# Gate/up projection: the even blocks 2 to 8 take three of their eight k-pairs by seven products

## The chip, the cores and the metric

The kernel runs on one core of a Trainium2 chip. The metric is the device time of one execution in microseconds (us); of several runs the median is given. TensorE (PE in the profile) multiplies, VectorE (DVE), ScalarE (ACT) and GpSimd (POOL) do the element-wise work, and SyncE (SP) issues most of the transfers from memory.

## The reference

One decoder layer on 256 tokens of width 2048, all in float32. Only the two feed-forward parts are touched by the change; each has gate and up projections of 2048 x 5632 and a down projection of 5632 x 2048.

```
def swiglu(x, w_gate, w_up, w_down):
    return (jax.nn.silu(x @ w_gate) * (x @ w_up)) @ w_down

def reference(x, ...):
    x = x + 0.5 * swiglu(rms_norm(x, ffn1_norm), ffn1_w_gate, ffn1_w_up, ffn1_w_down)
    ...   # projection w_in, gated linear attention, dilated attention, projection w_out
    x = x + 0.5 * swiglu(rms_norm(x, ffn2_norm), ffn2_w_gate, ffn2_w_up, ffn2_w_down)
    return x
```

## The kernel before

**Numbers.** Each float32 operand is split into a high and a low part (`wh`, `wl` for weights, `hh`, `hl` for activations), and a product is the sum of high x high, high x low and low x high: three matmuls. `split` is one ScalarE copy (L115, writes the high part) followed by one VectorE subtraction (L116, writes the low part), so every weight passes through both engines before TensorE can use it.

**Tiling of gate and up.** The 5632 columns are 11 blocks of 512 columns of gate and 512 of up (`b` = 0 to 10). The 2048 rows are 16 tiles of 128, taken two at a time: 8 k-pairs to a block, here called pairs 0 to 7. One transfer of 1 MB (L221, on SP's queue) brings one pair's weights into a buffer `raw`; there are three such buffers, so the transfer for a pair is issued when VectorE and ScalarE are done with the pair three before it. Weight tiles `wh`, `wl` have `WBUF` = 4 buffers each.

**A plain pair** is two weight tiles, so two L115 and two L116 of 128x1024, and 24 matmuls of 512 columns: two row tiles, two token halves, gate and up, three matmuls each.

**A pair by seven products** treats two row tiles by two token halves times two row tiles by gate and up as a 2 x 2 product of blocks and takes 7 instead of 8 block products: 21 matmuls. For it `seven` prepares four weight tiles in the steps "plain" (the sum L242, two additions L245 into `room["more"]`, and the split of the middle two), "last" (a split of 128x512 into the single pair of tiles `swh`, `swl`), "sums" (the split of what L242 wrote), and "more" (the split of what both L245 wrote, by one ScalarE copy). All of them are VectorE and ScalarE work. Seven sums of products end in banks `ms`, which `fold` adds up after the block's last such pair (L490 on ScalarE, L491, L492, L493 on VectorE), and `evac` takes the block's result out (L456, L458, L459 on VectorE, L457 on ScalarE, then the 32x32 transposes L130, small transfers L137 on GpSimd's queue, and the split into `uh`, `ul`).

**Which pairs.** A text per block says it, `s` for a plain pair and `g` for one by seven products; `_order` numbers the `g` ones first:

```
FF_SEVEN = range(1, 11)
FF_THREE = range(1, 10, 2)
FF_ORDERS = [_order("ssgsggss" if b in FF_THREE else "ssgssgss" if b in FF_SEVEN else "ssssssss") for b in range(FF // 512)]
```

So block 0 is plain, the odd blocks 1 to 9 have three pairs by seven products (pairs 2, 4 and 5), and the even blocks 2 to 10 two (pairs 2 and 5). The accumulator banks change sides from block to block.

**What sets the order.** `weights()` keeps two to three weight tiles prepared ahead of their use; `later` holds pieces of other work that are handed out step by step. The program's builder then orders the instructions of each engine by a planned time line of its own. In the trace VectorE's instructions start in exactly the order of its list, so one that waits holds up all behind it.

Of the kernel before, what the change touches and what calls it, by code (L numbers as in the profile page):

```python
# [28 lines left out]
EPS = 1e-6  # L29
WBUF = 4  # L30
FF_SEVEN = range(1, 11)
FF_THREE = range(1, 10, 2)
TAIL = 4
WARM = 10
GH, GDK, GDV, RANK = 4, 128, 256, 16
# [4 lines left out]
def _order(text):  # L40

    seven, plain = iter(range(text.count("g"))), iter(range(text.count("g"), len(text)))
    return [(next(seven), True) if c == "g" else (next(plain), False) for c in text]


FF_ORDERS = [_order("ssgsggss" if b in FF_THREE else "ssgssgss" if b in FF_SEVEN else "ssssssss") for b in range(FF // 512)]
DOWN_ORDERS = [_order("ssssssgssgssgsgsgsgsss"), _order("sgsssgssgssgssgsgsssss")]
# [947 lines left out]
```

## Time and profile before

| | |
|---|---|
| median of 3 runs (lowest to highest) | 1713.23 us (1711.72 to 1714.13) |
| the profiled execution: its time, its span | 1712.98 us, 1711.2 us |
| granted TensorE clock | 0.999 |
| TensorE busy | 1701.1 us, 99%, 7944 records |
| VectorE busy | 1451.1 us, 85%, 1775 instructions |
| ScalarE busy | 964.8 us, 56% |
| GpSimd busy | 506.4 us, 30% |
| gate/up blocks 1 to 9, first feed-forward part | about 52 to 411 us of the span |
| gate/up blocks 1 to 9, second feed-forward part | about 1088 to 1446 us of the span |

A busy time is the time in which at least one instruction of the engine was in execution; matmuls overlap, so TensorE's busy time says little, and the spacing of their starts says more. Times in the rows below count from the start of the span. A row of the time line has the start, the duration, the engine, the line of the kernel, the operation, what it writes and reads, the shapes, a count, and in brackets the idle time of its engine before it and what ended that. `PE`, `DVE`, `ACT`, `POOL` and `SPq` are TensorE, VectorE, ScalarE, GpSimd and SyncE's queue.

### The profile page before, as it was taken

How to read it: one execution, taken by the hardware profiler on the slowest of the kernel's cores; microseconds unless marked ns; L12 is line 12 of the kernel's file. 1: busy time of each engine (PE TensorE's matmuls, PEld its weight loads, DVE VectorE, ACT ScalarE, POOL GpSimd, SP SyncE). 2: the span in 40 equal slices, each digit the busy share in tenths (PEclk: the TensorE clock that was granted, in tenths of full speed). 3: DMA queues.
4: the chain of work that ended last, by engine and by line, in shares of the span. 5: the costliest groups of instructions: out<-in, count | busy, mean ns of one | idle time of the engine just before them, and what ended most of it. 6: DMA issues, size and time to landing. Idle time of an engine off the chain costs nothing.

```text
span 1711.2 us, 22342 instructions
## 1 busy us (share of the span) xinstructions
PE 1701.1 (99%) x7944; PEld 1480.4 (87%) x7944; DVE 1451.1 (85%) x1775; ACT 964.8 (56%) x1195; POOL 506.4 (30%) x1002
## 2 busy tenths in 40 slices
PE   9999999999999999999999999999999999999999
PEld 7888888888888888888888888888888888888887
DVE  6989999999899788577865788899998999898876
ACT  7656565565555555564654555556555655555453
POOL 0333334343500511064250033343333333420000
PEclk9999999999999999999999999999999999999999
DMA  8566656566665656567564457666666666665654
GB/s 342 213 227 225 224 209 235 209 238 213 237 247 222 216 203 243 195 230 242 191 208 170 152 193 261 227 224 222 231 224 228 227 213 220 223 250 225 242 203 148
DMA packets 85809, 378.63 MB, mean 221 GB/s; under 512 B 21393, under 2 KB 38801, under 8 KB 42689
## 3 DMA queue, kind: packets, MB, share of 16 engines
q1 hardware_dynamic: 50864, 350.25, 57.2%
q0 software_dynamic: 34112, 25.88, 5.4%
q8 instruction: 62, 1.02, 0.2%
q10 hardware_dynamic: 720, 1.07, 0.2%
q14 instruction: 51, 0.41, 0.1%
HBM read 354.57 MB, written 4.19 MB: 210 GB/s over the span
## 4 chain that ended last, share of the span: by engine, by line
PE 92%; DMA 3%; DVE 3%; POOL 2%; issue 1%; ACT 0%; SPq 0%; DVEq 0%; ACTq 0%; POOLq 0%
PE acc L284 20%; PE acc L286 20%; PE acc L282 20%; PE acc L308 5%; PE acc L309 5%; PE acc L307 5%; PE tp L286 4%; PE tp L284 4%; PE tp L282 4%; DVE wl L116 1%; PE tp L309 1%; PE tp L308 1%; PE tp L307 1%; DMA hh<-us 1%; POOL hh L137 1%
## 5 line engine op out<-in xcount | busy, mean ns | idle before, releaser
L115 ACT ACTIVATE wh<-raw 128x1024 fp32r<-128x1024 f32 (+2 forms) x610 | 631.1, 1048 | 443.5 <-PE acc L286 194.2
L116 DVE TENSOR_TENSOR wl<-raw,wh 128x1024 fp32r<-128x1024 f32 (+1 forms) x608 | 732.2, 1218 | 147.9 <-ACT wh L115 145.3
L137 POOL DMA_DIRECT2D xs<-us x704 | 344.5, 497 | 545.9 <-DVE us L130 289.9
L286 PE MATMUL acc<-wh,hl 128*128 128x512 f32 x1192 | 359.8, 381 | 0.0
L284 PE MATMUL acc<-wl,hh 128*128 128x512 f32 x1192 | 358.9, 381 | 0.1
L282 PE MATMUL acc<-wh,hh 128*128 128x512 f32 x1192 | 349.0, 381 | 2.2 <-ACT wh L115 1.9
L282 PEld LDWEIGHTS acc<-wh,hh 128*128 128x128 f32 x1192 | 225.0, 189 | 36.4 <-ACT wh L115 3.0
L284 PEld LDWEIGHTS acc<-wl,hh 128*128 128x128 f32 x1192 | 225.3, 189 | 33.0 <-issue 0.7
L286 PEld LDWEIGHTS acc<-wh,hl 128*128 128x128 f32 x1192 | 225.6, 190 | 32.1 <-DVE hl L551 0.2
L115 ACT ACTIVATE wh<-xs 128x1024 fp32r<-128x1024 f32 x100 | 105.6, 1056 | 104.1 <-DVE xs L245 33.1
L116 DVE TENSOR_TENSOR wl<-xs,wh 128x1024 fp32r<-128x1024 f32 x100 | 120.8, 1218 | 2.4 <-ACT wh L115 2.4
L284 PE MATMUL acc<-wl,uh 128*128 128x512 f32 x384 | 117.4, 380 | 0.4 <-DVE wl L116 0.4
L286 PE MATMUL acc<-wh,ul 128*128 128x512 f32 x384 | 117.0, 379 | 0.0
L282 PE MATMUL acc<-wh,uh 128*128 128x512 f32 x384 | 112.2, 380 | 0.7 <-ACT wh L115 0.7
L137 POOL DMA_DIRECT2D hh<-us x128 | 62.2, 505 | 128.5 <-DVE us L130 68.2
L242 DVE TENSOR_TENSOR xs<-raw 128x1024 f32<-128x1024 f32 x50 | 61.3, 1225 | 29.7 <-DMA raw<-in_w_ff_dram 29.7
L282 PEld LDWEIGHTS acc<-wh,uh 128*128 128x128 f32 x384 | 72.3, 189 | 12.4 <-ACT wh L115 2.3
L284 PEld LDWEIGHTS acc<-wl,uh 128*128 128x128 f32 x384 | 72.3, 189 | 11.8 <-DVE wl L116 1.8
L286 PEld LDWEIGHTS acc<-wh,ul 128*128 128x128 f32 x384 | 72.6, 189 | 10.3
L245 DVE TENSOR_TENSOR xs<-xs,raw 128x512 f32<-128x512 f32 x100 | 68.7, 687 | 0.4
L282 PE MATMUL tp<-wh,hh 128*128 128x512 f32 x200 | 61.6, 379 | 0.0
L286 PE MATMUL tp<-wh,hl 128*128 128x512 f32 x200 | 59.5, 379 | 0.0
(325 smaller groups left out, 2474.7 us busy)
## 6 DMA issues: line engine op xcount, KB each, us to landing
raw<-in_w_ff_dram SPq DMA_DIRECT2D x175, 1024.0 KB, 5.1
raw<-in_w_dn_dram SPq DMA_DIRECT2D x88, 1024.0 KB, 4.9
raw<-in_w_mix_dram SPq DMA_DIRECT2D x48, 1024.0 KB, 4.9
raw<-in_w_out_dram SPq DMA_DIRECT2D x16, 1024.0 KB, 4.9
xs<-us POOLq DMA_DIRECT2D x704, 16.0 KB, 4.0
xs<-in_x_dram SPq DMA_DIRECT2D x2, 1024.0 KB, 9.3
xs<-in_x_dram POOLq DMA_DIRECT2D x2, 1024.0 KB, 5.5
hh<-us POOLq DMA_DIRECT2D x128, 16.0 KB, 3.8
```

Of the source, the lines that this page charges most:

```text
L115: nc.scalar.activation(dst_h, src, AF.Copy)
L116: nc.vector.tensor_sub(dst_l, src, dst_h.bitcast(F32))
L137: nc.gpsimd.dma_start(dst[32 * q:32 * q + 32, ..., r * n:(r + 1) * n], src[32 * r:32 * r + 32, ..., q * n:(q + 1) * n])
L242: nc.vector.tensor_add(room["sum"], b1, mid)
L245: nc.vector.tensor_add(room["more"][:, j, :], b, raw[:, 1, j, :])
L282: nc.tensor.matmul(ps[j], lhsT=sh, rhs=alt(wh[:, j, :]), start=first and i == 0, stop=False)
L284: nc.tensor.matmul(ps[j], lhsT=sh, rhs=alt(wl[:, j, :]), start=False, stop=False)
L286: nc.tensor.matmul(ps[j], lhsT=sl, rhs=alt(wh[:, j, :]), start=False, stop=last and i == len(ws) - 1)
L307: nc.tensor.matmul(bank, lhsT=a[0], rhs=alt(ws[0][:, j, :]), start=start, stop=False)
L308: nc.tensor.matmul(bank, lhsT=a[0], rhs=alt(ws[1][:, j, :]), start=False, stop=False)
L309: nc.tensor.matmul(bank, lhsT=a[1], rhs=alt(ws[0][:, j, :]), start=False, stop=stop)
```

## The change

The set of blocks with three such pairs becomes 1 to 9, so blocks 2, 4, 6 and 8 also take pair 4 by seven products. That is four pairs in each of the two feed-forward parts, eight in all.

```
-FF_THREE = range(1, 10, 2)
+FF_THREE = range(1, 10)
```

In the built program TensorE has 24 matmuls fewer, VectorE 40 instructions more and ScalarE 16 more; the transfers of SP and GpSimd are the same in number. The builder also orders VectorE's list anew, in the blocks that had three before as well. Two places of it follow, both in block 5 of the first feed-forward part (an odd block, three such pairs before and after). The numbers behind the names count buffers.

The first place is VectorE's work for pair 5, the last of the three, from its sum L242 to its last split ("more", the second `wl<-xs_78` after the two L245). Before:

```order
L242 TENSOR_TENSOR xs_78<-raw_2110 128x1024
L245 TENSOR_TENSOR xs_78<-xs_78,raw_2110 128x512
L116 TENSOR_TENSOR wl_2116<-raw_2110,wh_2115 128x1024
L245 TENSOR_TENSOR xs_78<-xs_78,raw_2110 128x512
L116 TENSOR_TENSOR swl_511<-raw_2110,swh_510 128x512
L116 TENSOR_TENSOR wl_2134<-xs_78,wh_2133 128x1024
L116 TENSOR_TENSOR ul_126<-xs_78,uh_125 128x4x128
L116 TENSOR_TENSOR wl_2144<-xs_78,wh_2143 128x1024
```

The same place after:

```order
L242 TENSOR_TENSOR xs_78<-raw_2122 128x1024
L116 TENSOR_TENSOR wl_2116<-xs_78,wh_2115 128x1024
L116 TENSOR_TENSOR wl_2128<-raw_2122,wh_2127 128x1024
L245 TENSOR_TENSOR xs_78<-xs_78,raw_2122 128x512
L116 TENSOR_TENSOR swl_511<-raw_2122,swh_510 128x512
L116 TENSOR_TENSOR wl_2146<-xs_78,wh_2145 128x1024
L245 TENSOR_TENSOR xs_78<-xs_78,raw_2122 128x512
L116 TENSOR_TENSOR ul_126<-xs_78,uh_125 128x4x128
L116 TENSOR_TENSOR wl_2156<-xs_78,wh_2155 128x1024
```

The second L245 moved back behind the split of the sums: one instruction (`ul`) stands between it and the split that needs its result, where three stood before. (`wl_2116<-xs_78` in the second row is pair 4's "more", which comes after pair 5's L242 now.)

The second place is VectorE's work at the end of the block, from pair 7's splits to L242 of the next block's pair 2. The buffer that this L242 reads (`raw_2334` before, `raw_2346` after) is the one that pair 7 held, three pairs earlier. Before:

```order
L116 TENSOR_TENSOR wl_2163<-raw_2150,wh_2162 128x1024
L491 TENSOR_TENSOR xs_78<-xs_78,acc_2017 128x512
L116 TENSOR_TENSOR wl_2175<-raw_2172,wh_2174 128x1024
L492 TENSOR_TENSOR xs_78<-xs_78,acc_2018 128x512
L116 TENSOR_TENSOR wl_2195<-raw_2172,wh_2194 128x1024
L493 TENSOR_TENSOR xs_78<-xs_78,acc_2016 128x2x512
L116 TENSOR_TENSOR wl_2215<-raw_2212,wh_2214 128x1024
L116 TENSOR_TENSOR wl_2231<-raw_2212,wh_2230 128x1024
L242 TENSOR_TENSOR xs_78<-raw_2334 128x1024
```

After:

```order
L116 TENSOR_TENSOR wl_2175<-raw_2162,wh_2174 128x1024
L116 TENSOR_TENSOR wl_2187<-raw_2184,wh_2186 128x1024
L491 TENSOR_TENSOR xs_78<-xs_78,acc_2029 128x512
L116 TENSOR_TENSOR wl_2207<-raw_2184,wh_2206 128x1024
L492 TENSOR_TENSOR xs_78<-xs_78,acc_2030 128x512
L116 TENSOR_TENSOR wl_2227<-raw_2224,wh_2226 128x1024
L493 TENSOR_TENSOR xs_78<-xs_78,acc_2028 128x2x512
L116 TENSOR_TENSOR wl_2243<-raw_2224,wh_2242 128x1024
L242 TENSOR_TENSOR xs_78<-raw_2346 128x1024
```

L491 and L492 moved one place back, so that L492 now stands between pair 7's last split, which frees the buffer, and the L242 that waits for it to be filled again. In blocks 3 to 9 of the first part and 4 to 9 of the second, pair 5's "more" follows its second L245 with `ul` alone between, and at the ends of the same blocks L492 stands behind pair 7's last split. At the ends of blocks 1 and 2 (1 to 3 in the second part) the order is still that from before.

## Prediction

> **What bounds the kernel now.** I read the page's busy shares first, then the windows of single blocks, then VectorE's time line at a block's end. The first fence has lines of the page (groups end with: busy us, mean ns of one | idle time before them). It shows a TensorE that is hardly ever idle and a VectorE at 85%; that is an average over stages, so the gate/up blocks have to be looked at alone.
>
> ```profile
> PE 1701.1 (99%) x7944; PEld 1480.4 (87%) x7944; DVE 1451.1 (85%) x1775; ACT 964.8 (56%) x1195; POOL 506.4 (30%) x1002
> L115 ACT ACTIVATE wh<-xs 128x1024 fp32r<-128x1024 f32 x100 | 105.6, 1056 | 104.1 <-DVE xs L245 33.1
> L242 DVE TENSOR_TENSOR xs<-raw 128x1024 f32<-128x1024 f32 x50 | 61.3, 1225 | 29.7 <-DMA raw<-in_w_ff_dram 29.7
> L245 DVE TENSOR_TENSOR xs<-xs,raw 128x512 f32<-128x512 f32 x100 | 68.7, 687 | 0.4
> ```
>
> The next fence has four windows. The first two run from TensorE's first low-part matmul of block 5 to that of block 6, and on to block 7's. The last two run from VectorE's L242 of pair 2 in block 5 to that of block 6, and on to block 7's.
>
> ```profile
> core 0: us, PE busy (x) PEld busy (x) DVE busy (x) ACT busy (x) POOL busy (x), PEclk, DMA share, GB/s
> 211.81:251.31 39.50, 39.50 (x185) 34.59 (x183) 37.48 (x42) 24.79 (x28) 15.63 (x32) 1.00 0.64 226
> 251.31:291.45 40.14, 40.14 (x187) 35.15 (x186) 36.66 (x43) 21.90 (x25) 15.66 (x32) 1.00 0.64 224
> ...
> 209.19:250.22 41.03, 41.03 (x191) 35.91 (x191) 39.01 (x45) 25.43 (x29) 15.63 (x32) 1.00 0.64 222
> 250.22:289.00 38.78, 38.78 (x181) 33.97 (x180) 35.31 (x39) 21.41 (x24) 15.66 (x32) 1.00 0.64 227
> ```
>
> TensorE needs 39.50 us for an odd block (183 matmuls) and 40.14 for an even one (186): 0.216 us each, without a stop. VectorE needs 41.03 us for an odd block, longer than TensorE, and 38.78 for an even one. So VectorE falls behind by 41.03 - 39.50 = 1.53 us in each odd block and makes up for it in the even one. TensorE leads the kernel only because every second block lets VectorE recover.
>
> The reason for the 41.03 is in VectorE's time line at the end of block 5 (start, duration, instruction, idle time before it).
>
> ```profile
> 237.27 0.69 DVE L116 TENSOR_TENSOR ul<-xs,uh 128x512 fp32r<-128x512 f32 x1
> 237.88 1.22 DVE L116 TENSOR_TENSOR wl<-xs,wh 128x1024 fp32r<-128x1024 f32 x1
> 239.01 2.35 DVE L116 TENSOR_TENSOR wl<-raw,wh 128x1024 fp32r<-128x1024 f32 x2
> 241.28 0.68 DVE L491 TENSOR_TENSOR xs<-xs,acc 128x512 f32<-128x512 f32 x1
> 241.88 1.22 DVE L116 TENSOR_TENSOR wl<-raw,wh 128x1024 fp32r<-128x1024 f32 x1
> 243.01 0.69 DVE L492 TENSOR_TENSOR xs<-xs,acc 128x512 f32<-128x512 f32 x1
> 243.61 1.22 DVE L116 TENSOR_TENSOR wl<-raw,wh 128x1024 fp32r<-128x1024 f32 x1
> 244.74 1.22 DVE L493 TENSOR_TENSOR xs<-xs,acc 128x1024 f32<-128x1024 f32 x1
> 245.88 2.36 DVE L116 TENSOR_TENSOR wl<-raw,wh 128x1024 fp32r<-128x1024 f32 x2
> 250.22 1.23 DVE L242 TENSOR_TENSOR xs<-raw 128x1024 f32<-128x1024 f32 x1 [1.98 <-DMA raw<-in_w_ff_dram]
> ```
>
> The 1.98 us are the only wait in that stretch; the work is 41.03 - 1.98 = 39.05 us, 0.45 less than TensorE's 39.50. The wait is a loop of VectorE's own: the split at 243.61 frees pair 7's buffer at 244.83, the next transfer into it lands 5.4 us later, and in between VectorE has 3.4 us of work. A later VectorE frees the buffer later, so the wait doesn't shrink when VectorE is behind. In a row, instructions start 1.14 us (128x1024) and 0.60 us (128x512) apart.
>
> The Trainium skill (VectorE: DVE Perf Modes, the section on the TRN2 errata) gives an fp32 add of N columns (N + 151)/0.96 ns, 691 and 1224 ns. The rows' single durations agree (687, 1225), but in a row the starts are closer; by the page an odd block's 44 instructions would take about 42.8 us (an estimate) instead of the 39.05 seen, and the loss below would be some 50 us. The trace decides, and the sum goes by 39.05.
>
> **How much room there is.** I call "lead" the time from L242 of a block's pair 2 on VectorE to TensorE's first low-part matmul (L284) of that block. The next rows give it for block 5 of the first part and block 2 of each part, and the first use of pair 6's low part.
>
> ```profile
> 209.19 1.23 DVE L242 TENSOR_TENSOR xs<-raw 128x1024 f32<-128x1024 f32 x1 [0.47 <-DMA raw<-in_w_ff_dram]
> 211.81 0.38 PE L284 MATMUL acc<-wl,hh 128*128 128x512 f32 x1
> 241.38 0.38 PE L284 MATMUL acc<-wl,hh 128*128 128x512 f32 x1
> ...
> 90.23 1.23 DVE L242 TENSOR_TENSOR xs<-raw 128x1024 f32<-128x1024 f32 x1 [1.31 <-DMA raw<-in_w_ff_dram]
> 92.02 0.38 PE L284 MATMUL acc<-wl,hh 128*128 128x512 f32 x1
> ...
> 1126.07 1.23 DVE L242 TENSOR_TENSOR xs<-raw 128x1024 f32<-128x1024 f32 x1 [1.36 <-DMA raw<-in_w_ff_dram]
> 1127.58 0.38 PE L284 MATMUL acc<-wl,hh 128*128 128x512 f32 x1
> ```
>
> Block 5 has a lead of 2.62 us. Pair 6's first low part is ready at 239.01 + 1.22 = 240.23 and used at 241.38, 1.15 us later. A block with three such pairs therefore needs a lead of 2.62 - 1.15 = 1.47 us, or TensorE waits. Block 2, the first that changes, has 1.79 in the first part and 1.51 in the second: just enough.
>
> **The change part by part.**
>
> TensorE: 24 matmuls fewer; per block 40.14 - 39.50 = 0.64 us, eight blocks, 5.1 us less.
>
> VectorE: 40 instructions more, five for each new pair, which turn an even block's work into an odd one's, 39.05 us. Every block from 2 to 9 then has 39.50 us of TensorE against 39.05 us of VectorE and its waits. More than 0.45 us of waits per block is lost, with no lighter block behind it to win it back.
>
> First wait, L242 at the block's end. In the eight odd blocks 3 to 9 of both parts it was (the row of 250.22 above is the eighth):
>
> ```profile
> 170.42 1.23 DVE L242 TENSOR_TENSOR xs<-raw 128x1024 f32<-128x1024 f32 x1 [1.70 <-DMA raw<-in_w_ff_dram]
> 330.68 1.23 DVE L242 TENSOR_TENSOR xs<-raw 128x1024 f32<-128x1024 f32 x1 [2.63 <-DMA raw<-in_w_ff_dram]
> 409.29 1.22 DVE L242 TENSOR_TENSOR xs<-raw 128x1024 f32<-128x1024 f32 x1 [1.41 <-DMA raw<-in_w_ff_dram]
> 1206.18 1.22 DVE L242 TENSOR_TENSOR xs<-raw 128x1024 f32<-128x1024 f32 x1 [1.51 <-DMA raw<-in_w_ff_dram]
> 1285.23 1.22 DVE L242 TENSOR_TENSOR xs<-raw 128x1024 f32<-128x1024 f32 x1 [1.31 <-DMA raw<-in_w_ff_dram]
> 1365.02 1.22 DVE L242 TENSOR_TENSOR xs<-raw 128x1024 f32<-128x1024 f32 x1 [1.47 <-DMA raw<-in_w_ff_dram]
> 1444.89 1.23 DVE L242 TENSOR_TENSOR xs<-raw 128x1024 f32<-128x1024 f32 x1 [1.70 <-DMA raw<-in_w_ff_dram]
> ```
>
> The mean is 13.71 / 8 = 1.71 us. It stays where the end of the block keeps its order. Where L492 now stands inside the loop, 0.60 us more work covers it: 1.11. But with L492 gone from before the split, pair 6's buffer and pair 7's are freed 1.14 + 0.60 + 1.14 = 2.88 us apart instead of 3.47 (244.83 less the end of the two splits from 239.01), and transfers close behind each other land late:
>
> ```profile
> L221 SPq DMA_DIRECT2D raw<-in_w_ff_dram x74: 327/328/328, 66.8 to 430.9; - x74
> 66.78 2.67 SPq L221 DMA_DIRECT2D raw<-in_w_ff_dram  x2
> raw<-in_w_ff_dram SPq DMA_DIRECT2D x1, 1024.0 KB, 5.7
> ...
> raw<-in_w_ff_dram SPq DMA_DIRECT2D x16, 1024.0 KB, 5.0
> ```
>
> The first row says that an issue takes 0.33 us; the second is two issues, so 2.67 - 0.33 = 2.34 us apart; the third is what the later of them took until it landed, the fourth the median of 16 transfers in blocks 5 and 6. So the wait lies between 1.11 and 1.71, and 1.30 is taken, nearer the lower end, as 2.88 lies between a spacing that cost 0.7 us and one that cost next to nothing.
>
> Second wait, ScalarE in the middle of pair 5. "More" needs the second L245 (0.69 us), then ScalarE's copy (1.06), then VectorE. That is 1.75 us and two hand-overs. One shows where VectorE waits for a copy at the end of block 4 (the copy ends at 206.40 + 1.06 = 207.46, the split starts at 207.49):
>
> ```profile
> 206.40 1.06 ACT L115 ACTIVATE wh<-raw 128x1024 fp32r<-128x1024 f32 x1 [1.53 <-PE acc L286]
> 207.49 1.23 DVE L116 TENSOR_TENSOR wl<-raw,wh 128x1024 fp32r<-128x1024 f32 x1 [0.76 <-ACT wh L115]
> ```
>
> With 0.03 for each it is 1.81 us, and with one `ul` between (0.60 + 0.60) VectorE has only 1.20 us to fill it and waits 0.61. At pair 4's "more" an L242 lies between (1.74), another 0.07: 0.68 in all, in blocks 3 to 9 (4 to 9 in the second part); 0.07 alone in the block before these. Its ends are nothing, if the copy starts sooner than I think, and 1.06, the whole copy. As it lies ahead of pair 6, the needed lead becomes 1.47 + 0.68 = 2.15.
>
> SP's and GpSimd's transfers are the same, and PSUM's fold and evacuation keep their distance, as VectorE is later and TensorE not; I cost them at nothing. If `ul` had to wait for GpSimd's transfers, the price would go to the second wait.
>
> The sum: block 2 loses 39.05 + 1.71 + 0.07 - 39.50 = 1.33 us of lead in the first part and 1.26 in the second, whose block 3 loses 1.33. Each later block loses 39.05 + 0.68 + 1.30 - 39.50 = 1.53. First part: 1.79 - 1.33 - 6 x 1.53 = -8.72 at block 9, where 2.15 are needed: TensorE waits 10.87. Second: 1.51 - 1.26 - 1.33 - 5 x 1.53 = -8.73: it waits 10.88. Block 10 keeps its two such pairs and VectorE recovers there. Together 21.75 of waits against 5.1 saved: +16.6 us. The profiled execution took 1712.98 us (span 1711.2), 0.25 below the median of 1713.23; with the median the forecast is 1729.8.
>
> **The rivals.**
>
> TensorE stays the bound (0.07). The saving is kept whole if a block's waits come to less than 0.45 us, for example if L242's wait only looks long because VectorE, four weight tiles ahead, had to wait there anyway. 1713.2 - 5.1 = 1708.1, faster. For it: at the end of block 5 VectorE is at its furthest ahead. Against it: block 6 started with 1.53 us less lead, and all eight waits are over 1.3. The Trainium skill (DMA: Bandwidth & Descriptors, "Rules for kernel authors") speaks for this rival: a transfer that is issued early, with work between it and its wait, overlaps its fixed cost. The trace agrees in part only: 3.4 us of work lie over a 5.4 us round trip, and 1.98 us stay bare.
>
> Break-even (0.10). The shortest wait, 1.31, shortened by the whole 0.60, and no ScalarE wait: 0.26 lost per block, 4 to 6 us of stalls in all against 5.1 saved, 1713.
>
> VectorE leads, but without the ScalarE wait (0.15): each block loses 0.85 and the lead needed is 1.47. First part -0.32 + 1.26 + 6 x 0.85 = 6.0, second -0.04 + 2.52 + 4.25 = 6.7, less 5.1: 1720.9.
>
> It gets worse (0.10). With the longest L242 wait (2.63 - 0.60 = 2.03) in each of the eleven later blocks the loss is 2.26 instead of 1.53 each, 8.0 us on top: 1737.8.
>
> **How the numbers follow.** The forecast's case, VectorE the bound with both waits, has 0.58: 1729.8, from 1723 to 1737. What a measurement of this kernel can tell from no change is about 0.2%, 3.4 us. Faster by more: the first rival, 0.07. Same: the break-even case, 0.10. Slower: 0.58 + 0.15 + 0.10 = 0.83. The range reaches from 1717, below the case without the ScalarE wait, to 1739, above the case of the longest L242 waits; 0.17 lies below it.
>
> **What would show it.** In the profile after: blocks 4 to 9 take about 41.0 us each on both engines; TensorE waits some 1.5 us per block, ended by VectorE's or ScalarE's splits at pairs 4 to 6; L242 of pair 2 still waits 1.1 to 1.7 us; "more" of pair 5 waits 0.6 us for ScalarE. Blocks of 39.5 us and no waits on TensorE would prove the forecast wrong; blocks near 40.3 would say that the ScalarE wait isn't there.

## The result and the profile after

The changed kernel took 1726.66 us (median of 6 runs, 1723.98 to 1728.39) and the kernel before, on the same chip, 1712.79 us (6 runs, 1711.68 to 1714.13): a ratio of 1.0082, with a 95% interval of 1.0072 to 1.0093, so 13.9 us slower. The prediction was 1729.8 us, slower. The profiled execution took 1728.39 us, with a span of 1726.6 us; before it was 1712.98 and 1711.2. The medians and ratios of this document are over executions at full speed: of the seven of the kernel e1 below, two are left out (2226.09 us at a granted clock of 0.752, and 7877.36 us), and one of eighteen of the kernel before beside it (3362.31 us).

The page's lines that answer to the first fence of the prediction:

```profile
PE 1704.2 (99%) x7920; PEld 1471.8 (85%) x7920; DVE 1481.9 (86%) x1815; ACT 970.1 (56%) x1211; POOL 506.4 (29%) x1002
L115 ACT ACTIVATE wh<-xs 128x1024 fp32r<-128x1024 f32 x116 | 122.5, 1056 | 165.2 <-DVE xs L245 119.7
L242 DVE TENSOR_TENSOR xs<-raw 128x1024 f32<-128x1024 f32 x58 | 70.8, 1220 | 25.5 <-DMA raw<-in_w_ff_dram 25.4
L245 DVE TENSOR_TENSOR xs<-xs,raw 128x512 f32<-128x512 f32 x116 | 79.2, 683 | 0.2
```

TensorE is still "99% busy", because the ends of its matmuls are modelled; that number hides the whole loss. What moved is ScalarE's idle time before the copies that wait for an L245: 119.7 us, where it was 33.1; that idle time costs nothing by itself, but VectorE's split behind such a copy comes later by it. L242's wait for raw transfers fell in total (25.4 after 29.7), though there are more of them.

The same four windows as before: two from TensorE's first low-part matmul of block 5 to that of blocks 6 and 7, two from VectorE's L242 of pair 2 to the next.

```profile
core 0: us, PE busy (x) PEld busy (x) DVE busy (x) ACT busy (x) POOL busy (x), PEclk, DMA share, GB/s
212.49:253.35 40.86, 40.24 (x185) 34.61 (x184) 37.93 (x44) 23.08 (x27) 15.65 (x32) 1.00 0.65 221
253.35:295.18 41.83, 40.36 (x184) 34.03 (x183) 39.94 (x45) 24.00 (x29) 15.66 (x32) 1.00 0.62 212
211.22:253.25 42.03, 41.41 (x191) 35.64 (x190) 39.10 (x44) 23.63 (x27) 15.65 (x32) 1.00 0.65 220
253.25:294.25 41.00, 39.53 (x180) 33.31 (x179) 39.11 (x45) 23.45 (x28) 15.66 (x32) 1.00 0.62 213
```

TensorE's blocks are now as long as VectorE's (40.86 and 41.83 against 42.03 and 41.00), and no longer 39.50. VectorE works 39.1 us in each and waits for the rest. Its time line shows both waits, at pair 5's "more" and at the next L242:

```profile
238.74 0.69 DVE L245 TENSOR_TENSOR xs<-xs,raw 128x512 f32<-128x512 f32 x1
239.34 0.69 DVE L116 TENSOR_TENSOR ul<-xs,uh 128x512 fp32r<-128x512 f32 x1
240.63 1.22 DVE L116 TENSOR_TENSOR wl<-xs,wh 128x1024 fp32r<-128x1024 f32 x1 [0.60 <-ACT wh L115]
...
249.78 1.22 DVE L116 TENSOR_TENSOR wl<-raw,wh 128x1024 fp32r<-128x1024 f32 x1
253.25 1.23 DVE L242 TENSOR_TENSOR xs<-raw 128x1024 f32<-128x1024 f32 x1 [2.26 <-DMA raw<-in_w_ff_dram]
```

And TensorE's time line shows where it stops in that block, at pair 5's last products and the first of pair 6:

```profile
240.65 0.48 PE L307 MATMUL acc<-wh,uh 128*128 128x512 f32 x1 [0.37 <-ACT wh L115]
241.59 0.70 PE L282 MATMUL acc<-wh,hh 128*128 128x512 f32 x2 [0.24 <-ACT wh L115]
```

The idle times in these two rows are too small, again because ends are modelled. Counted from the starts instead (what exceeds the usual 216 ns from one matmul to the next, called TensorE's waits from here on), TensorE waited 11.11 us in the first part's gate/up blocks and 11.15 in the second's; before it was 0.23 and 0.

### The profile page after: what moved, and what is told of

It is laid out like the page before. It is cut to its first block, busy times and chain, and to the rows that moved or that the text cites. A ratio compares the mean times of both kernels' runs of the same rounds, so it can differ in the third digit from the quotient of the medians.

```text
span 1726.6 us, 22379 instructions
## 1 busy us (share of the span) xinstructions
PE 1704.2 (99%) x7920; PEld 1471.8 (85%) x7920; DVE 1481.9 (86%) x1815; ACT 970.1 (56%) x1211; POOL 506.4 (29%) x1002
## 3 DMA queue, kind: packets, MB, share of 16 engines
q10 hardware_dynamic: 720, 1.07, 0.2%
## 4 chain that ended last, share of the span: by engine, by line
PE 75%; DVE 10%; DMA 8%; issue 3%; POOL 2%; ACT 2%; DVEq 0%; ACTq 0%; SPq 0%; POOLq 0%
PE acc L284 16%; PE acc L286 16%; PE acc L282 16%; DVE wl L116 5%; DMA xs<-us 4%; PE acc L308 4%; PE acc L309 4%; PE acc L307 4%; PE tp L286 4%; PE tp L284 4%; PE tp L282 3%; DMA raw<-in_w_ff_dram 2%; POOL xs L137 2%; ACT wh L115 1%; PE tp L308 1%
## 5 line engine op out<-in xcount | busy, mean ns | idle before, releaser
L115 ACT ACTIVATE wh<-raw 128x1024 fp32r<-128x1024 f32 (+1 forms) x602 | 621.0, 1046 | 403.4 <-PE acc L286 182.2
L286 PE MATMUL acc<-wh,hl 128*128 128x512 f32 x1128 | 340.8, 381 | 0.0
L284 PE MATMUL acc<-wl,hh 128*128 128x512 f32 x1128 | 340.3, 380 | 0.1
L282 PE MATMUL acc<-wh,hh 128*128 128x512 f32 x1128 | 333.3, 383 | 5.3 <-ACT wh L115 4.9
L282 PEld LDWEIGHTS acc<-wh,hh 128*128 128x128 f32 x1128 | 211.5, 189 | 42.8 <-ACT wh L115 12.9
L284 PEld LDWEIGHTS acc<-wl,hh 128*128 128x128 f32 x1128 | 212.8, 189 | 31.3 <-DVE wl L116 0.9
L286 PEld LDWEIGHTS acc<-wh,hl 128*128 128x128 f32 x1128 | 213.0, 189 | 30.1
L115 ACT ACTIVATE wh<-xs 128x1024 fp32r<-128x1024 f32 x116 | 122.5, 1056 | 165.2 <-DVE xs L245 119.7
L116 DVE TENSOR_TENSOR wl<-xs,wh 128x1024 fp32r<-128x1024 f32 x116 | 140.7, 1213 | 9.7 <-ACT wh L115 8.6
L242 DVE TENSOR_TENSOR xs<-raw 128x1024 f32<-128x1024 f32 x58 | 70.8, 1220 | 25.5 <-DMA raw<-in_w_ff_dram 25.4
L245 DVE TENSOR_TENSOR xs<-xs,raw 128x512 f32<-128x512 f32 x116 | 79.2, 683 | 0.2
L457 ACT ACTIVATE sg<-sg,rt 128x512 f32<-128x512 f32 x40 | 29.0, 724 | 67.3 <-DVE sg L456 67.3
```

What stands on the lines that cost most here:

```text
L115: nc.scalar.activation(dst_h, src, AF.Copy)
L116: nc.vector.tensor_sub(dst_l, src, dst_h.bitcast(F32))
L242: nc.vector.tensor_add(room["sum"], b1, mid)
L245: nc.vector.tensor_add(room["more"][:, j, :], b, raw[:, 1, j, :])
L282: nc.tensor.matmul(ps[j], lhsT=sh, rhs=alt(wh[:, j, :]), start=first and i == 0, stop=False)
L284: nc.tensor.matmul(ps[j], lhsT=sh, rhs=alt(wl[:, j, :]), start=False, stop=False)
```

## The experiments

The theory to be tested: VectorE is the bound in a row of three-pair blocks, because to its 39.1 us of work come two waits which the order of its list makes: at L242 for the raw transfer, and at "more" for ScalarE. The rivals: one of the two waits alone makes the loss; or the additional VectorE work does, whatever the order.

For each kernel stands one row of windows over four blocks of the first part (from L242 of pair 2 in block 5 to that in block 9; columns as above). VectorE's idle time is the length less "DVE busy", the fourth number with a count of about 177. For the changed kernel:

```profile
211.22:375.51 164.29, 160.82 (x734) 137.40 (x733) 156.41 (x176) 94.32 (x108) 62.62 (x128) 1.00 0.63 218
```

164.29 / 4 = 41.07 us per block, of which 39.10 is work and 1.97 waiting. All comparisons below are with the kernel before on the same chip.

### e1: the first sum not put ahead

```
-                nc.vector.tensor_add(room["sum"], b1, mid)
+                add = nc.vector.tensor_add(room["sum"], b1, mid); "more" in room and tc.keep_in_program_order(add)
```

> Edit: in the blocks of three k-pairs the first sum of a pair (L242) may not be put ahead of what is written before it, so that 9.3 us of VectorE work instead of 4.0 stand between the release of the raw buffer and the sum that waits for its next filling; the same work otherwise. The new order puts 0.60 us instead of 1.20 and more between the second L245 and the split that needs it, in pairs 4 and 5. Theory (VectorE bound, two waits of the order): the wait for the raw transfer goes to under 0.3 us per block (1.4 in the changed kernel), the wait for ScalarE grows from 0.68 to about 2.4 us (twice 1.81 - 0.60), so VectorE needs 39.05 + 2.4 = 41.5 us per block where the changed kernel needed 41.1: about 1727 us or a little slower, 1722 to 1736. Rival (the raw transfer alone makes the loss): 1709 us. Rival (the loss is VectorE work alone, whatever the order): 1726.7, no wait moved.

Measured: 1753.39 us, ratio 1.0237 (1.0223 to 1.025). The profile that is read here is of a further execution of the same kernel.

> The kernel of the run e1 again, for a profile at full clock. In its order the split of the fourth matrix (swl, L116), which reads the same raw buffer, stands ahead of the first sum of pair 2, where the changed kernel has the sum: so the wait for the raw transfer may not be gone but handed to that split, by way of ScalarE's copy. Theory: VectorE waits 1.0 to 2.0 us per block at swl for ScalarE, whose copy waits for the raw transfer, and about 2.4 us per block at the two splits behind the second L245; together 3 to 4 us per block, 1752 to 1756 us. Rival (no wait at swl; all of the loss at the splits behind L245): those hold over 3 us per block.

That execution took 1753.72 us. The window, and three rows of VectorE's time line that hold all its idle time from 340 to 386 us:

```profile
219.93:389.00 169.07, 161.88 (x733) 137.06 (x733) 156.78 (x178) 94.82 (x109) 62.56 (x128) 1.00 0.61 212
```

```profile
344.39 1.23 DVE L116 TENSOR_TENSOR wl<-raw,wh 128x1024 fp32r<-128x1024 f32 x1 [0.63 <-ACT wh L115]
367.42 1.23 DVE L116 TENSOR_TENSOR wl<-xs,wh 128x1024 fp32r<-128x1024 f32 x1 [1.21 <-ACT wh L115]
375.66 1.23 DVE L116 TENSOR_TENSOR wl<-xs,wh 128x1024 fp32r<-128x1024 f32 x1 [1.21 <-ACT wh L115]
```

The first wait is gone, and not handed to `swl` either: that guess of the second run was wrong. The second wait grew to 2 x 1.21 = 2.42 us, as worked out (1.81 - 0.60, twice). Two things were missed. One is a wait of 0.63 us in every block at the first split of pair 1, which neither theory had (see e4). The other is an error in my sum for e1: 1727 compared VectorE's 41.5 us per block with the changed kernel's 41.1, but there the first blocks of a part live on their lead, and here nearly every block loses 42.27 - 39.50 = 2.77 us from the first on. TensorE's waits in e1's gate/up blocks are 24.1 us in the first part and 23.7 in the second; less the 5.1 of matmuls that is 42.7 us, and 41.9 were measured (1753.39 - 1711.49). The raw transfer alone doesn't make the loss.

### e2: the second L245 ahead of the fourth matrix

```
-                        nc.vector.tensor_add(room["more"][:, j, :], b, raw[:, 1, j, :])
+                        room["pin"] = nc.vector.tensor_add(room["more"][:, j, :], b, raw[:, 1, j, :]).ins
 ...
-                wh, wl = room["wh"], room["wl"]
-                split(wh[:, 0, :], wl[:, 0, :], raw[:, 1, 1, :])
+                with tc.issue_after(room["pin"]) if "more" in room else ExitStack():
+                    split(room["wh"][:, 0, :], room["wl"][:, 0, :], raw[:, 1, 1, :]); wh, wl = room["wh"], room["wl"]
```

> Edit: in the blocks of three k-pairs the split of the fourth matrix (the one called last) stays behind the second L245 on VectorE and ScalarE, so that 1.8 to 3.5 us of VectorE work stand between the second L245 and the split that needs it, where 1.81 are needed; L242 of pair 2 stays where it is. Theory: the wait for ScalarE goes from 0.68 us per block to under 0.1, the wait of L242 for its raw transfer stays near 1.4; VectorE needs 40.5 instead of 41.1 us per block, the loss against TensorE's 39.50 falls from about 1.55 to about 0.95: TensorE's waits fall from 22.3 to about 13 us, 1718 us (1714 to 1723). Rival (the raw transfer alone makes the loss): 1726.7, unchanged. Rival (ScalarE alone): 1709.

Measured: 1717.29 us, ratio 1.0029 (1.0018 to 1.004). The window and the waits of VectorE in it:

```profile
209.47:371.51 162.04, 160.44 (x733) 137.00 (x732) 156.05 (x177) 95.72 (x109) 62.83 (x128) 1.00 0.63 221
```

```profile
engine line waited for: us in total, times, longest us
DVE xs L242 <- DMA raw<-in_w_ff_dram: 7.4, 5, 2.1
```

The wait for ScalarE is gone and the other stays: L242 waited 1.48, 2.09, 1.47, 0.94 and 1.42 us in a row (five, since the window takes in both ends). 162.04 / 4 = 40.51 us per block, and TensorE's waits fell from 22.3 to 12.5 us. So the wait of 0.68 us per block for ScalarE, the smaller of the two, is worth some 8 us of the changed kernel's 13.9 (1717.29 - 1711.49 = 5.8 are left): both rivals with a single wait fall.

### e3 and e4: both waits

e3 holds both orders of e1 and e2. e4 holds a third, the split of the sums behind the second L245:

```
-                wh, wl = wtile("wh"), wtile("wl")
-                split(wh, wl, room["sum"])
+                wh, wl = wtile("wh"), wtile("wl"); pin = tc.issue_after(room["pin"]) if "more" in room else ExitStack()
+                with pin: split(wh, wl, room["sum"])
```

> Edit: both of the two orders. 8.1 us of VectorE work stand between the release of the raw buffer and the first sum that waits for its next filling; 1.9, 1.2 and 1.8 us between the second L245 and its split in pairs 2, 4 and 5. Theory: no wait for the raw transfer, 0.6 us per block for ScalarE in pair 4; VectorE needs 39.05 + 0.6 = 39.65 us against TensorE's 39.50: at most 0.15 us lost per block, TensorE's waits in both parts together under 3 us, and of the 5.1 us of matmuls saved nearly all is seen: 1709 us, 1707 to 1712. Rival (VectorE's work is too much at any order, because its instructions take longer than the 39.05 us of single durations once nothing waits): 1720 and more.

> Edit: as the run before, and the split of the sums too stays behind the second L245: 3.0, 2.3 and 2.3 us between the second L245 and its split. Theory: neither wait is left, VectorE needs 39.05 us, less than TensorE's 39.50, TensorE's waits under 1 us in both parts: the time before less the matmuls saved, 1712.8 - 5.1 = 1707.7 us, 1706 to 1710. Rival (the work alone is too much): 1720 and more. Rival (the first blocks' start costs what the order saves): 1711 to 1714.

Measured: e3 1721.22 us, ratio 1.005 (1.0038 to 1.0062); e4 1714.70 us, ratio 1.0016 (1.0008 to 1.0025). Both are some 7 to 12 us above what the theory gave, and the rival "the work alone is too much" isn't it either: in e4's window VectorE works 156.78 / 4 = 39.20 us per block and waits 0.91. Nor is it e4's third rival, a loss in the first blocks: the window below is of blocks 5 to 8, and they take 160.40 / 4 = 40.10 us each.

```profile
212.71:373.11 160.40, 160.14 (x733) 137.38 (x733) 156.78 (x177) 97.21 (x108) 62.82 (x128) 1.00 0.64 223
```

VectorE's waits in e4 from 314 to 330 us, from its time line:

```profile
314.97 0.69 DVE L116 TENSOR_TENSOR ul<-xs,uh 128x512 fp32r<-128x512 f32 x1 [0.17 <-ACT uh L115]
328.94 1.23 DVE L116 TENSOR_TENSOR wl<-raw,wh 128x1024 fp32r<-128x1024 f32 x1 [0.67 <-ACT wh L115]
```

The ScalarE copies ahead of the second of them, then two matmuls of TensorE ahead of which it stood still and the first that uses the split of 328.94:

```profile
322.67 1.06 ACT L115 ACTIVATE wh<-raw 128x1024 fp32r<-128x1024 f32 x1 [0.89 <-PE tp L286]
325.26 1.06 ACT L115 ACTIVATE wh<-raw 128x1024 fp32r<-128x1024 f32 x1 [1.53 <-PE tp L286]
327.85 1.06 ACT L115 ACTIVATE wh<-raw 128x1024 fp32r<-128x1024 f32 x1 [1.53 <-PE tp L286]
```

```profile
316.92 0.48 PE L308 MATMUL acc<-swl,hh 128*128 128x512 f32 x1
318.05 0.48 PE L308 MATMUL acc<-wl,uh 128*128 128x512 f32 x1
...
335.85 0.59 PE L284 MATMUL acc<-wl,hh 128*128 128x512 f32 x2
```

At 316.92 TensorE takes up `swl` of pair 5 in the moment in which VectorE has written it: there VectorE is late. Twelve us later, at 328.94, VectorE is too early: ScalarE's copies follow each other every 2.59 us, the time of 12 matmuls, since each has to wait until TensorE has left one of the four `wh` buffers, and VectorE waits behind them. So VectorE can't save up more lead than four weight tiles hold, and spends more than that later in the block. From the end of a split to the first use of its result, the longest lead in this stretch of e4 is that of the split of 328.94: it ends at 330.17 and is used at 335.85, 5.68 us later. (The expectations of f1 and f3 below take 4.03 us for the longest, which is the lead of a tile three earlier.) A pair by seven products takes 4 x 1.14 + 3 x 0.60 = 6.36 us of VectorE, and 1.07 us for its eighth of the block's remaining work, against 4.54 on TensorE: it uses up 2.9 us of lead. Pairs 4 and 5 in a row use 5.8, and pair 2 has taken 2.9 before them, of which the plain pair 3 gives 1.8 back. The waits that the prediction named are gone in e4, and this third limit, which it had not, keeps 40.10 - 39.50 = 0.6 us per block; the account of it is worked out here and tried in f1. In e3 VectorE still waits 0.61 us per block for ScalarE at pair 4, and its blocks take 40.41 us.

### c4: the same orders on the kernel before

> Edit: the kernel before with the three orders of the run e4 (first sum not put ahead, the fourth matrix and the sums split behind the second L245), so its odd blocks alone have three pairs of seven products. Theory (TensorE is the bound before, so an order of VectorE can't gain): 1712 us, within 4 us of before, no gain over 2 us; if the order holds VectorE back in the odd blocks too (e4 lost 0.6 us per block against TensorE's 39.50), the rest of an even block gives it back. Rival (the orders are a gain of their own, not the repair of a wait that the change brought): 1707 or less.

Measured: 1714.74 us, ratio 1.0015 (1.0006 to 1.0024). The orders bring nothing by themselves (the kernel is 2.5 us slower with them), so what they win back in e2 to e4 is what the change had lost.

### f1, f3, f5: the three pairs further apart

```
-FF_ORDERS = [_order("ssgsggss" if b in FF_THREE ...
+FF_ORDERS = [_order("ssgsgsgs" if b in FF_THREE ...
 ...
-                        if folds:
+                        for _ in range(min(len(folds), 1 if odd is None or span else 2)):
                             folds.pop(0)()
```

These are the edits of f1 on top of e4. f3 has the text `sgssgsgs`, f5 `sgsgsgss` (and the folds as they were).

> Edit: e4, and the three pairs of seven products are pairs 2, 4 and 6 of a block instead of 2, 4 and 5 (the four folds behind the last of them run two to a step, since two plain products are left for them). What e4 left: its VectorE had no wait for a transfer or an L245, yet waited 0.67 us per block at the start of pair 1 for ScalarE, which waited for TensorE to free one of the four wh buffers; and TensorE waited 0.6 us per block at pair 5 for VectorE. Theory (a run of two pairs needs more lead than the four buffers hold): a pair of seven takes VectorE 6.36 us of its own and 1.07 of the rest of the block, against 21 x 0.216 = 4.54 on TensorE, so it uses up 2.9 us of lead; a plain pair (2.28 + 1.07 against 5.18) gives 1.8 back; pairs 4 and 5 in a row use 5.8, and the longest lead in e4 is 4.03. With a plain pair between them the use is 3.95 at most over two and 5.0 over three: TensorE's waits fall from 0.6 to 0.0 to 0.3 us per block, 1706 to 1711 us, 1709 at a guess. Rival (VectorE is simply too slow at 39.1 to 39.3 us of work and the gaps of 35 ns): 1714.7 as e4. Rival (two plain products are too few for the folds, and the next block's first products wait for them): 1716 to 1730.

> Edit: as f1 with the pairs 1, 4 and 6, the widest spacing that a block allows with two plain pairs between the first and the second. Theory (lead): the use over any run is 3.95 us at most, under the 4.03 that the buffers hold: waits of TensorE under 0.2 us per block, 1707 us, 1705 to 1710. Rival (the seven sums' four banks are not free yet at pair 1, 5.2 us after the block's start, since the block before is still read out of them by L456 and L458, of which the last begins 6.7 us after a block's start in e4): a wait of up to 1.5 us plus the products behind it, 1715 to 1735.

> Edit: e4 with the pairs 1, 3 and 5 (the folds as they were). Theory (lead): 3.95 us over two, 5.0 over three, then three plain pairs in a row that give 5.5 back: as f1 without its short time for the folds, 1706 to 1711 us. Rival (the banks at pair 1): a wait of up to 1.5 us per block, 1715 to 1735. Rival (spacing does nothing): 1714.7.

f1 took 1707.15 us (1704.75 to 1708.63) against 1712.25 us: a ratio of 0.9968 (0.9955 to 0.998), the only kernel here that beats the one before.

```profile
213.06:371.05 157.99, 157.99 (x734) 138.35 (x733) 156.78 (x178) 96.86 (x108) 62.82 (x128) 1.00 0.65 227
```

```profile
DVE xs L491 <- ACT wh L115: 0.8, 4, 0.2
```

157.99 / 4 = 39.50: TensorE's own time, with the same 156.78 us of VectorE work as in e4. VectorE's only wait is 0.2 us per block. TensorE doesn't stop once in blocks 1 to 9 of either part. The 5.1 us that the change saves in matmuls are there: 1712.25 - 1707.15 = 5.1, with an interval of 3.4 to 7.7. f1 also runs two folds to a step where e4 runs one; a kernel with that alone was not run, but TensorE's waits, which the spacing was to remove, are gone.

f3 took 1787.16 us, ratio 1.0434 (1.042 to 1.0448), and f5 1758.17 us, ratio 1.0274 (1.0257 to 1.0291). Their rival had the place, pair 1 behind the evacuation of the block before, but not the cause, and its "up to 1.5 us" is under half of the wait in f3. In f3, VectorE and TensorE at pair 1 of the block that begins at 314 us:

```profile
319.64 0.75 DVE L459 SCALAR_TENSOR_TENSOR u<-xs,rt,sg 128x512 f32<-128x512 f32 x1 [0.79 <-ACT sg L457]
320.43 0.71 DVE L130 STREAM_TRANSPOSE us<-u 128x512 f32<-128x512 f32 x1
321.06 1.18 DVE L242 TENSOR_TENSOR xs<-raw 128x1024 f32<-128x1024 f32 x1
```

```profile
320.01 0.38 PE L307 MATMUL acc<-swh,hh 128*128 128x512 f32 x1
323.47 1.22 PE L307 MATMUL acc<-wh,fh 128*128 128x512 f32 x2 [3.08 <-ACT wh L115]
```

The first sum of pair 1 comes behind the whole evacuation of the block before (L456, L457, L459, L130), and TensorE's next matmul starts 3.46 us after the one before: a wait of 3.24 us, which ends with ScalarE's copy of that sum and not with a bank that comes free. (In f5 the wait at pair 1 is 1.62 us in most blocks.) Whether the held order puts it there or the room that the sums share with the evacuation was not separated. In these kernels the spacing is worth something only where the first of the three pairs leaves time for the evacuation.

### f2 and f8: which parts of f1 are needed

> Edit: the changed kernel with the pairs 2, 4 and 6 instead of 2, 4 and 5 (and two folds to a step), none of the three held orders. The spacing alone lets the written order come out with 5.8 us instead of 4.0 of VectorE work between the raw buffer's release and the first sum, and 3.0, 1.7 and 2.3 us between the second L245 and its split. Theory (two waits of the order, and a run of two pairs that needs more lead than the buffers hold): the wait for the raw transfer at most 0.5 us per block, the wait for ScalarE 0.1, VectorE at 39.05 to 39.6 us per block against 39.50: as f1, 1707 us, 1704 to 1711. Rival (the held orders are what brought f1 to 1707, and spacing only adds to them): 1715 to 1722.

> Edit: f2 with the first of the held orders alone (L242 not put ahead), which brings 7.5 us of work ahead of the first sum, but only 1.2 and 0.6 us between the second L245 and its split in pairs 4 and 6. Theory: no wait for the transfer and no run of two pairs, but a wait for ScalarE of 0.61 + 1.21 = 1.8 us per block, so VectorE needs 40.9 against 39.50 us: 1.3 to 1.4 lost per block after the first one or two, 10 to 11 us in a part, about 1728 us, 1720 to 1735. Rival (a short distance to the split costs nothing where the pairs are spaced, since each wait is made good in the plain pair behind it): 1707 to 1711.

Both missed, theory and rival alike. f2 took 1740.63 us, ratio 1.017 (1.0156 to 1.0184); f8 1753.36 us, ratio 1.0246 (1.0232 to 1.026). The distances in f2's expectation are those of pair 2 alone. Its window, and the two rows with idle time between 317 and 337 us:

```profile
216.31:383.54 167.23, 162.62 (x734) 136.66 (x733) 156.45 (x178) 94.66 (x109) 62.58 (x128) 1.00 0.62 214
```

```profile
323.11 1.23 DVE L242 TENSOR_TENSOR xs<-raw 128x1024 f32<-128x1024 f32 x1 [1.58 <-DMA raw<-in_w_ff_dram]
335.23 1.22 DVE L116 TENSOR_TENSOR wl<-raw,wh 128x1024 fp32r<-128x1024 f32 x1 [0.54 <-ACT wh L115]
```

The L242 at 323.11 is pair 6's: it stands ahead of pair 5's splits and waits there for its raw transfer. The first wait is the same, at another pair. In f8, where the sum is held back, the split of the fourth matrix took its place at pair 6, and waited for the same transfer by way of ScalarE (VectorE's rows with idle time from 320 to 340 us, then ScalarE's copy):

```profile
326.08 0.69 DVE L116 TENSOR_TENSOR swl<-raw,swh 128x512 fp32r<-128x512 f32 x1 [1.21 <-ACT swh L115]
327.03 1.23 DVE L116 TENSOR_TENSOR wl<-xs,wh 128x1024 fp32r<-128x1024 f32 x1 [0.26 <-ACT wh L115]
336.94 1.23 DVE L116 TENSOR_TENSOR wl<-xs,wh 128x1024 fp32r<-128x1024 f32 x1 [1.20 <-ACT wh L115]
```

```profile
325.42 0.63 ACT L115 ACTIVATE swh<-raw 128x512 fp32r<-128x512 f32 x1 [2.84 <-DMA raw<-in_w_ff_dram]
```

These three and 0.19 us at L459 make 2.9 us per block, where 1.8 was expected: the wait for ScalarE (0.26 + 1.20) is some 0.3 less than that, and the 1.21 for the transfer wasn't forecast. So neither the spacing (f2, 1741) nor the held orders (e4, 1715) give f1's 1707 alone, and in both kernels the instruction that now reads the raw buffer first, put ahead, brings the first wait back.

### x1: more VectorE work, no wait

```
+            room.get("n", 0) % 3 == 1 and part == "more" and "more" in room and nc.vector.tensor_sub(wl, room["more"], wh.bitcast(F32)); ...
```

> Edit: f1 with one subtraction of 128x1024 written twice in each block (the same values into the same place: 1.14 us more of VectorE work per block, no wait added). Theory (the three-pair block leaves VectorE only some 0.2 us of room: in f1 it was idle 0.20 us per block of 39.50): 0.9 us lost per block once the lead is used up, which f1 shows as 0.97 us at the closest place: 0.9 x 9 - 1 = 7 us in a part, 1721 us, 1714 to 1724. Rival (VectorE isn't the bound, only its waits were): 1707, unchanged.

Measured: 1717.37 us, ratio 1.0034 (1.0021 to 1.0046).

```profile
215.15:377.07 161.92, 159.75 (x734) 137.57 (x733) 160.92 (x181) 94.69 (x108) 62.62 (x128) 1.00 0.65 221
```

160.92 - 156.78 = 4.14 us more work in four blocks, and the blocks became 0.98 us longer each (40.48 against 39.50). One additional subtraction per block costs 11 us of the kernel: x1 is 5.9 us above before, f1 was 5.1 below. VectorE's room in a three-pair block is no more than the 0.3 us per block (157.99 - 156.78 over four) that f1 leaves.

## Why the prediction was right, point by point

- **VectorE's work, 39.05 us per block:** 39.10 in the changed kernel's window. TensorE's saving of 5.1 us was real, and is seen whole in f1.
- **First wait.** 1.30 us was taken for the eleven later block ends, 1.38 was measured (15.13 / 11). That is luck in part: only two of the eleven, 1.21 and 1.71, lie within the bounds I gave, 1.11 to 1.71. They go by how long the transfer took to land after the split that frees its buffer: 4.8 to 5.2 us in seven cases, 5.7 in one and 6.2 in three. I had laid late landing to transfers issued 2.88 us apart. In all eleven cases the issues are 2.87 us apart, so that spacing doesn't decide it. The row of 253.25 above is of the slowest sort, this one from VectorE's time line of the fastest:

```profile
334.82 1.22 DVE L242 TENSOR_TENSOR xs<-raw 128x1024 f32<-128x1024 f32 x1 [0.80 <-DMA raw<-in_w_ff_dram]
```

  The mean came out because the slow ones (waits of 2.21 to 2.26 us) make up for the fast (0.80 to 1.21). What decides between the two stays open. At the three block ends that kept their order 1.71 was taken, and 1.34, 1.59 and 1.55 were measured.
- **Second wait.** 0.61 us was worked out for pair 5, 0.60 was measured, with 0.07 at pair 4, 0.67 to 0.68 in all, in each block where the order has it. e2 took it away, and the time fell to 1717.3 us; the rival "without the ScalarE wait" had 1720.9 for that case.
- **The sum.** TensorE's waits: 10.87 and 10.88 us forecast, 11.11 and 11.15 measured. Blocks 4 to 9: about 41.0 us forecast, 40.95 and 41.14 measured on average, from L242 to L242. TensorE waits at the splits of pair 5, as said.
- **What was off.** The net was 16.6 us, against 15.4 between the two profiled executions. The waits were 0.5 larger, 0.2 of them were there before as well, and the rest of the kernel, which I costed at nothing, was 1.5 us shorter (its start 1.5 and its middle 1.4 shorter, its end 1.3 longer). In the start the kernel before ran 3.4 us at half the granted clock, from 15.1 us on, and the changed kernel didn't, which is a difference of the two executions. The median lies another 1.7 us below the profiled execution. None of that belongs to the mechanism, and that these differences are small and partly cancel is luck.
- **The rivals.** "TensorE stays the bound" supposed that VectorE, four tiles ahead, had to wait at the block's end anyway. The mechanism exists, but in the changed kernel VectorE has no lead to be stopped by. It showed once the two waits were gone, in e4. I had not counted it on the other side: with both waits repaired the change still gave no gain, as two of its pairs stand in a row.

## What to carry to other kernels

When an edit makes an engine nearly the bound (here 39.1 us of work in 39.5), the order of its list can decide the sign: count each wait that the order makes, per block, against the room that is left, and expect nothing to be made good where the lighter blocks are gone. A total that fits isn't enough: work has to be spread so that no stretch uses up more lead than the buffers between the engines can hold. If a wait is repaired by holding one instruction back, look at what takes its place ahead of the others, since it may wait for the same thing.

## What the runs showed of the hardware

TensorE's granted clock fell after a short stop. In f3, windows around the wait of 3.24 us (the number behind POOL's is the granted clock):

```profile
312.00:320.00 8.00, 8.00 (x38) 7.00 (x38) 6.98 (x10) 1.65 (x3) 1.19 (x3) 1.00 0.38 134
320.00:323.40 3.40, 0.39 (x2) 0.00 (x0) 3.30 (x5) 1.04 (x1) 3.40 (x8) 0.98 0.12 33
323.50:326.90 3.40, 3.40 (x9) 2.54 (x9) 3.40 (x5) 2.95 (x3) 3.40 (x8) 0.53 0.52 116
326.90:340.00 13.10, 13.10 (x62) 11.49 (x61) 11.45 (x13) 7.28 (x8) 7.60 (x16) 1.00 0.84 287
```

For 3.4 us after the wait matmuls started 0.427 us apart instead of 0.216, at a clock of 0.53, and then at full speed again: such a wait costs some 1.7 us more than its own length (a block lost 4.94 us there in all). The Trainium skill (TensorE: Matmul & The Clock Gate, "What's actually happening") says that the clock is halved after an idle window of about 3.4 us and given back after as long a busy one. The trace agrees on the 3.4 us at half clock, but the wait was 3.24 us, and f5 below shows that much less is enough. The Trainium skill (TensorE: Matmul & The Clock Gate, "Wait — 56ns, not 53.3ns?") gives spacings for 512 columns of 426.7 and 215.7 ns, and these are the ones seen here. I had not put this into the price of f3's and f5's rival.

In f5 a wait of 1.62 us was enough in some blocks and not in others:

```profile
142.05:145.46 3.41, 1.76 (x8) 0.69 (x6) 3.34 (x5) 2.19 (x3) 3.41 (x8) 1.00 0.12 33
145.46:148.87 3.41, 3.41 (x9) 2.78 (x9) 3.41 (x4) 2.81 (x4) 3.41 (x8) 0.50 0.86 274
...
186.42:189.83 3.41, 2.17 (x8) 1.20 (x9) 3.38 (x5) 3.02 (x4) 3.41 (x8) 1.00 0.28 55
189.83:193.24 3.41, 3.41 (x17) 3.01 (x16) 3.41 (x4) 2.42 (x3) 2.78 (x6) 1.00 0.82 317
```

Within f3 and within f5, the moments at which the clock fell in the gate/up blocks lie whole multiples of 3.413 us apart, so I count in stretches of that length that end on them (in f2 on its single fall). In the stretch before 145.46 TensorE's waits, with the short ones behind the long one, come to 2.21 us, and the next 3.41 us ran at half clock; in the stretch before 189.83 they come to 1.90, and the clock stayed. In the gate/up blocks of f2, f3 and f5 all 26 stretches with 2.18 us of waits or more were followed by half clock, and none at full clock with 1.90 or less. So in these three kernels it goes by how much of such a stretch is idle, and therefore also by where in it a wait falls; the limit between 1.90 and 2.18 us was not tried in a kernel of its own. The changed kernel's waits, 0.8 us at most each, show nothing of the kind; its clock reads 1.00 in every window above.
